# Residuals and norms handed over per stream, an output product by 128 tokens, and modulation as dot products on VectorE

## Chip, cores and metric

One core of one Trainium2 chip. The metric is the device time of one execution in microseconds, the median of several. Short names: PE is TensorE (PEld its weight loads), DVE is VectorE, ACT is ScalarE, POOL is GpSimd, SP is SyncE, whose queue issues nearly all the loads.

## The reference, cut to what matters

Two layers work on two streams of 256 tokens of width 1024: the context (stream 0 in the kernel) and the latent (stream 1). Each layer has a token mixer and a gated FFN with a width-3 convolution. Each of the two sub-layers is normed before and after, and modulated by six vectors of shift, scale and gate.

```python
sh1, sc1, g1, sh2, sc2, g2 = jnp.split((silu_c @ ada_w[layer] + ada_b[layer])[:, None, :], ADA_CHUNKS, axis=-1)
...
u_lat = rms_norm(h_lat, g_pre1) * (1.0 + sc1) + sh1
...
h_lat = h_lat + g1 * rms_norm(y_lat, g_post1)
v_lat = rms_norm(h_lat, g_pre2) * (1.0 + sc2) + sh2
h_lat = h_lat + g2 * rms_norm(conv_ffn(v_lat, w_ffn_in[layer], ...), g_post2)
```

The mixer ends in a product by w_out (1024x1024), the FFN in one by w_ffn_out (2816x1024). The context has the same chain with its own vectors; the second layer needs the context only as far as the mixer's keys and states, and has no FFN for it. The output is the latent stream.

## The kernel before

**Numbers and products.** Every f32 operand of a big product is split into a high part and a low part, and a product is three PE instructions (high by high, high by low, low by high). A chunk of weights is loaded by SP into one of five buffers called raw (line 246), copied by ACT to the high part wh (line 350), and the low part wl is formed by DVE (line 352); wh and wl have three buffers each. The casts are given with high priority. The kernel is written in a framework whose scheduler fixes each engine's instruction order ahead of the run, by priority (the order in which the program states the work, unless marked as urgent) and by when it reckons the operands ready. Each engine then works through its own list in that order.

**The token mixer's end.** `merge` (line 955) makes the merged tile mg. `outputs` (line 444) multiplies it by w_out in halves of 512 output columns: the first half for all streams together, then the second half stream by stream. In the second halves the last four k tiles are done token tile by token tile. Every weight chunk covers two k tiles. Lines 481 to 483 are the three instructions. After each half `post_half` (line 432) has ACT sum the squares (line 383) and DVE multiply by the gate row (line 436). The optional argument `fill` is a generator that is advanced once per weight chunk, in the first half only (line 455).

**Residual and norm.** In program order they come after all of `outputs`. `post_end` (line 438): POOL adds the two sums (line 441) and takes the power -1/2 (line 378), DVE adds the scaled result to the residual, 1024 columns at once (line 442). `norm_in` (line 414): ACT sums squares over 1024 columns (line 383), POOL adds and takes the power (lines 389, 378), ACT and DVE scale a half each into hn (lines 394, 395), and `prenorm` (line 397) has PE transpose it (line 405, urgent) into a PSUM bank for two column blocks, ACT write the modulated high part (line 409), DVE a copy of the modulated value (line 411), and DVE or POOL, in turn, the low part (line 412).

**The FFN.** `ffn_pair` (line 1006) is one of 22 column tiles. In the first layer the first three are done per stream with 256 tokens ("early pairs": context first, then its latent counterpart after the latent's norm), all the others for both streams at once. Then `outputs` does the FFN's own product, latent first. The context's FFN values are split in two when they are used (`inner`, line 1141): ACT the high part (line 1145), POOL the low part (line 1146).

**Modulation of later stages.** It has two forms. `ada_unit` (line 274) does 512 columns on PE: line 289, 128 columns at a time over 8 k tiles, then a copy, a transpose and small DVE steps (`ada_turn`). `ada_dots` (line 329) does one block of 128 columns per step: a load of 512 KB into a raw buffer and one DVE dot product per stream (line 338). One generator `ada` chains these. The first layer's runs through two units (the next layer's first shift), 8 + 8 blocks for the context and 8 + 32 for the latent; eight steps are taken before the early pairs, 2.7 per later pair, and the rest as `fill` in the FFN product. The second layer's is two units (its own last gate), all taken before its FFN.

**Between the layers.** `finish(1)` (line 1153) does the latent's residual and its norm for the next layer after the FFN product. `finish(0)` does the same for the context, called in the next layer after its first six projections, which need the latent only.

```python
        for g in groups:
            for t in range(2):
                self.post_end(*part[g, t], hs[g][t])
            self.norm_in(fp, l, g, hs[g], "A2", 24, v)
            for j in early:
                self.ffn_pair(l, fp, j, v, new(j), g * CTX, CTX, q0, True, j >= 2)
```

## Time and profile before

| what | value |
|---|---|
| median of 3 runs | 1571.18 us (1569.73 to 1573.08) |
| the profiled execution's own time | 1568.4 us |
| its span, first to last instruction | 1566.6 us |
| mean granted PE clock | 0.991 of full speed |
| PE busy | 1490.8 us, 95% |
| DVE busy | 1039.5 us, 66% |
| ACT busy | 738.4 us, 47% |
| POOL busy | 245.3 us, 16% |

The median carries what one can compare between kernels; the rows come from the one profiled execution, which was 2.8 us faster than the median. Its span leaves out 1.8 us of its own time. Positions in rows are microseconds from the span's start. The first layer's mixer output product is at 543 to 591, its FFN at 603 to 857, its FFN product at 857 to 986; the second layer's mixer output product is at 1328 to 1354, its FFN at 1367 to 1498, its FFN product at 1498 to 1559.

### The profile page before, as it was taken

The numbers are of one execution on the slowest core, as the hardware profiler recorded it, in microseconds if no ns is written. First come the engines' busy times: TensorE is split into PE (matmuls) and PEld (weight loads), VectorE is DVE, ScalarE is ACT, GpSimd is POOL, SyncE is SP. The second block draws the span as 40 slices with busy tenths as digits, with TensorE's granted clock in tenths as the row PEclk, the third lists the DMA queues.
The fourth block names the chain that finished last, engine by engine and source line by source line (L and its number), as shares of the span: only waits on it lengthen the run. The fifth ranks groups of instructions, "written<-read, shape, count | busy, mean of one in ns | idle before, by whom it ended". The sixth has DMA issues, their size and how long they took to land. (4 is left out here: it accounts for less than half of the span.)

```text
span 1566.6 us, 24172 instructions
## 1 busy us (share of the span) xinstructions
PE 1490.8 (95%) x9187; PEld 1279.0 (82%) x9187; DVE 1039.5 (66%) x1872; ACT 738.4 (47%) x1326; POOL 245.3 (16%) x335
## 2 busy tenths in 40 slices
PE   6999999999999998999999999899999989899997
PEld 5889877777777887888878886899997878799986
DVE  5546678778896457767776447646676787577754
ACT  3473334444444346332333346564455555455543
POOL 2101221001212223000000316401111123100000
PEclk9999999999999999999999999999999999899999
DMA  9321134333332356776665545422351334665553
GB/s 352 117 95 59 64 121 140 104 93 94 108 121 82 118 168 220 238 238 215 223 205 175 176 135 153 135 95 82 95 160 56 95 93 131 212 190 184 185 182 104
DMA packets 69717, 227.70 MB, mean 145 GB/s; under 512 B 7712, under 2 KB 8368, under 8 KB 69600
## 3 DMA queue, kind: packets, MB, share of 16 engines
q1 hardware_dynamic: 68000, 220.76, 43.9%
q0 software_dynamic: 1600, 5.39, 1.0%
q8 instruction: 72, 1.18, 0.3%
q14 instruction: 45, 0.37, 0.1%
HBM read 225.06 MB, written 1.06 MB: 144 GB/s over the span
## 5 line engine op out<-in xcount | busy, mean ns | idle before, releaser
L352 DVE TENSOR_TENSOR wl<-raw,wh 128x1024 fp32r<-128x1024 f32 (+6 forms) x333 | 385.7, 1163 | 181.5 <-ACT wh L350 180.0
L350 ACT CAST wh<-raw 128x1024 fp32r<-128x1024 f32 (+6 forms) x333 | 320.6, 966 | 239.0 <-PE mm L365 97.5
L364 PE MATMUL mm<-act,wh 128*128 128x256 f32 (+1 forms) x1096 | 372.7, 340 | 1.8 <-DVE ft L1020 1.6
L366 PE MATMUL mm<-act,wl 128*128 128x256 f32 (+1 forms) x1096 | 369.9, 338 | 4.2 <-DVE wl L352 4.1
L365 PE MATMUL mm<-act,wh 128*128 128x256 f32 (+1 forms) x1096 | 370.2, 338 | 0.2 <-POOL act L412 0.2
L366 PEld LDWEIGHTS mm<-act,wl 128*128 128x128 f32 x1096 | 209.5, 191 | 25.8 <-DVE wl L352 5.8
L364 PEld LDWEIGHTS mm<-act,wh 128*128 128x128 f32 x1096 | 209.7, 191 | 23.2 <-ACT wh L350 2.6
L365 PEld LDWEIGHTS mm<-act,wh 128*128 128x128 f32 x1096 | 209.7, 191 | 19.7 <-POOL act L412 0.4
L338 DVE CUSTOM_DVE_ANT_0 adot<-raw,srow,S 128x1024 bf16<-128x1024 f32 x104 | 134.0, 1289 | 73.5 <-DMA raw<-in_adat 67.4
L366 PE MATMUL ps<-act,wl 128*128 128x256 f32 (+1 forms) x328 | 109.3, 333 | 0.9 <-DVE wl L352 0.9
L364 PE MATMUL ps<-act,wh 128*128 128x256 f32 (+1 forms) x328 | 109.2, 333 | 0.0
L365 PE MATMUL ps<-act,wh 128*128 128x256 f32 (+1 forms) x328 | 109.2, 333 | 0.0
L483 PE MATMUL ps<-wh,al 128*128 128x512 f32 x198 | 78.8, 398 | 3.3 <-POOL al L1146 3.2
L579 PE MATMUL mm<-wh,act 128*128 128x272 f32 (+1 forms) x256 | 77.7, 304 | 1.6 <-ACT kb L770 1.6
L1022 ACT ACTIVATE ft<-ft 128x256 f32<-128x256 f32 (+1 forms) x47 | 23.7, 503 | 114.5 <-DVE ft L1020 90.4
L581 PE MATMUL mm<-wh,act 128*128 128x272 f32 (+1 forms) x256 | 77.0, 301 | 0.3 <-POOL act L412 0.3
L580 PE MATMUL mm<-wl,act 128*128 128x272 f32 (+1 forms) x256 | 76.8, 300 | 0.3 <-DVE wl L352 0.3
L1146 POOL TENSOR_TENSOR al<-ac,ah 128x256 fp32r<-128x256 f32 x44 | 41.7, 951 | 215.5 <-ACT ah L1145 215.4
L378 POOL TENSOR_TENSOR st<-st,mhalf 128x1 f32<-128x1 f32 (+3 forms) x56 | 48.8, 872 | 160.2 <-DVE st L606 123.5
L366 PEld LDWEIGHTS ps<-act,wl 128*128 128x128 f32 x328 | 62.6, 191 | 7.1 <-DVE wl L352 1.3
L364 PEld LDWEIGHTS ps<-act,wh 128*128 128x128 f32 x328 | 62.8, 191 | 6.0
L365 PEld LDWEIGHTS ps<-act,wh 128*128 128x128 f32 x328 | 62.6, 191 | 5.9
(300 smaller groups left out, 2830.5 us busy)
## 6 DMA issues: line engine op xcount, KB each, us to landing
raw<-in_wflat SPq DMA_DIRECT2D x253, 512.0 KB, 3.7
raw<-in_adat SPq DMA_DIRECT2D x80, 512.0 KB, 4.2
raw<-in_wflat SPq DMA_DIRECT2D x48, 256.0 KB, 2.7
araw<-in_ada SPq DMA_DIRECT2D x16, 512.0 KB, 7.2
raw<-in_ada SPq DMA_DIRECT2D x16, 512.0 KB, 3.9
raw<-in_wflat SPq DMA_DIRECT2D x8, 480.0 KB, 3.5
raw<-in_wflat SPq DMA_DIRECT2D x8, 408.0 KB, 3.2
raw<-in_wflat SPq DMA_DIRECT2D x8, 384.0 KB, 6.5
```

What stands on the lines that cost most here:

```text
L338: nc.vector.tensor_tensor_reduce(junk, r, rows[:, i], 1.0, self.S[l][:, L_AB + b:L_AB + b + 1], ALU.mult, ALU.add, self.MV[l][:, b, g:g + 1])
L350: nc.scalar.copy(h, raw)
L352: nc.vector.tensor_sub(lo, raw, h.bitcast(F32))
L364: self.nc.tensor.matmul(ps, a, xh(k), start=first and k == 0, stop=False)
L365: self.nc.tensor.matmul(ps, a, xl(k), start=False, stop=False)
L366: self.nc.tensor.matmul(ps, b, xh(k), start=False, stop=last and k == nk - 1)
L378: self.nc.gpsimd.tensor_tensor(r, ms, self.mhalf[:, :n], ALU.pow)
L483: self.nc.tensor.matmul(ps, xl, wh, start=False, stop=last)
L579: nc.tensor.matmul(ps, uh[:, k, tt], h[:, c], start=k == 0, stop=False)
L580: nc.tensor.matmul(ps, uh[:, k, tt], lo[:, c], start=False, stop=False)
L581: nc.tensor.matmul(ps, ul[:, k, tt], h[:, c], start=False, stop=k == KD - 1)
L1146: nc.gpsimd.tensor_sub(lo, a[k][0], h.bitcast(F32))
```

## The change

- `ada_unit` on PE is dropped. The first layer's generator has only dot products: 8 + 16 blocks for the context and 8 + 40 for the latent; none is taken before the early pairs, 2.5 per later pair, the rest as fill. The second layer's has its own 8 blocks for the latent, 0.5 per pair.
- `outputs` advances `fill` in the second halves too, and calls `done(g, ...)` as soon as a stream's second half is stated.
- `post_end` works in halves of 512 columns, each followed by a caller's step: the sum of squares of that half (`renorm`), or the store of that half (at the end).
- The first layer: the context's residual and normed tile are stated before the latent's second half, its transposes and modulation behind that half and before the latent's residual. Behind the FFN product the same, latent first; `finish()` only transposes and modulates the context.
- The second layer's mixer output product is done by `outputs_by_tile`: 128 tokens at a time, both halves; all eight chunks are loaded during tile 0, and seven of them have buffers of their own for wh and wl. Tile 0's normed tile is transposed (urgent) during tile 1 into four PSUM banks that tile 1 later completes.
- Of the context's low parts in the FFN product, the even k tiles go to DVE.

```diff
-    def weights(self, key, urgent=True):
+    def weights(self, key, urgent=True, pool=None):
...
-            h = self.wp.tile([P, WCH], F32R, tag="wh", name=self.nm("wh"))[:, :n]
+            new = lambda tag: (pool.tile([P, WCH], F32R, name=self.nm(tag)) if pool else self.wp.tile([P, WCH], F32R, tag=tag, name=self.nm(tag)))[:, :n]
+            h = new("wh")
             nc.scalar.copy(h, raw)
-            lo = self.wp.tile([P, WCH], F32R, tag="wl", name=self.nm("wl"))[:, :n]
+            lo = new("wl")
...
-    def post_end(self, s, yg, h):
+    def post_end(self, s, yg, h, after):
 
         ms = self.st(1)
         self.nc.gpsimd.tensor_scalar(ms, s[:, 0:1], s[:, 1:2], EPS, ALU.add, ALU.add)
-        self.nc.vector.scalar_tensor_tensor(h, yg, self.rstd(ms, 1), h, ALU.mult, ALU.add)
+        r = self.rstd(ms, 1)
+        for i in range(2):
+            c = slice(512 * i, 512 * i + 512)
+            self.nc.vector.scalar_tensor_tensor(h[:, c], yg[:, c], r, h[:, c], ALU.mult, ALU.add)
+            after(i, c)
+
+    def renorm(self, tp, s, yg, h):
+
+        q, ms = self.st(2), self.st(1)
+        self.post_end(s, yg, h, lambda i, c: self.square_sums(tp.tile([P, 512], F32, tag="ft", name=self.nm("jq"), bufs=2), h[:, c], q[:, i:i + 1]))
+        self.nc.gpsimd.tensor_scalar(ms, q[:, 0:1], q[:, 1:2], EPS, ALU.add, ALU.add)
+        hn = tp.tile([P, D], F32, tag="yg", name=self.nm("hn"), bufs=4)
+        self.scaled(hn, self.rstd(ms, 1), h)
+        return hn
...
-                if i == 0:
-                    next(fill, None)
+                next(fill, None)
...
+            done(g, [part[g, t] for t in range(2)])
+
+    def outputs_by_tile(self, key, x, tp, wp, gain, fill, done):
+
+        ws = {}
+        for t in range(2):
+            s, yg = self.st(2), tp.tile([P, D], F32, tag="yg", name=self.nm("yg"), bufs=4)
+            for i in (t, 1 - t):
+                y = self.mm()
+                for k in range(0, KD, 2):
+                    if t == 0:
+                        ws[i, k] = self.weights((*key, i, k), pool=wp if (i, k) != (1, KD - 2) else None)
+                        next(fill, None)
+                    for j in range(2):
+                        self.tokens_proj(y, [a[:, t * P:(t + 1) * P] for a in x(k + j)], [a[:, 512 * j:512 * j + 512] for a in ws[i, k]], k + j == 0, k + j == KD - 1)
+                self.post_half(tp, y, gain(), i, s, yg)
+            done(t, s, yg)
...
+        def wo_done(g, part):
+            if g:
+                for m in range(0, KD, 2):
+                    self.prenorm(fp, l, (m, m + 1), {0: hn[0]}, "A2", 24, v)
+            hn[g] = [self.renorm(fp, *part[t], hs[g][t]) for t in range(2)]
+
+        def tile_done(t, s, yg):
+            h = self.renorm(fp, s, yg, hs[1][t])
+            if t == 0:
+                hn[1] = [self.ps() for _ in range(KD // 2)]
+            for i, ps in enumerate(hn[1]):
+                self.turned(ps, (2 * i, 2 * i + 1), h, t)
...
-        for _ in range(8 if full else 12):
-            next(ada, None)
+        dots = lambda bs, g: self.ada_dots(fp, bs, (g,))
+        second = [(l, b) for b in range(40, 48)]
+        ada = chain(*(dots(second + [(l + 1, b) for b in range(40 if g else 16)], g) for g in range(2))) if full else dots(second, 1)
...
-                due += 2.7 if j < NF - 2 else 0
+                due += (2.5 if full else 0.5) if j < NF - 2 else 0
...
-            nc.gpsimd.tensor_sub(lo, a[k][0], h.bitcast(F32))
+            (nc.gpsimd if k % 2 else nc.vector).tensor_sub(lo, a[k][0], h.bitcast(F32))
...
+        def fo_done(g, part):
+            if not full:
+                for t in range(2):
+                    self.post_end(*part[t], hs[g][t], lambda i, c: nc.sync.dma_start(self.d["out"][t * P:(t + 1) * P, c], hs[g][t][:, c]))
+                return
+            hn[g] = [self.renorm(fp, *part[t], hs[g][t]) for t in range(2)]
+            if g:
+                normed(g)
+
+        def normed(g):
+            for m in range(0, KD, 2):
+                self.prenorm(fp, l + 1, (m, m + 1), {g: hn[g]}, "A1", 0, u)
+
+        def finish():
+            normed(0)
+            fst.close()
```

## Rows read from the trace of the kernel before

**Rows 1.** The page's head: span, and PE's busy time and share.

```profile
span 1566.6 us, 24172 instructions
...
PE 1490.8 (95%) x9187; PEld 1279.0 (82%) x9187; DVE 1039.5 (66%) x1872; ACT 738.4 (47%) x1326; POOL 245.3 (16%) x335
```

**Rows 2.** Busy time by stretch (length, engines, clock, DMA, GB/s), first layer, behind its output product.

```profile
591.00:603.50 12.50, 8.49 (x154) 6.32 (x147) 9.20 (x18) 9.32 (x19) 5.22 (x9) 1.00 0.83 301
603.50:622.20 18.70, 16.77 (x130) 15.45 (x128) 17.30 (x29) 13.66 (x21) 5.35 (x6) 1.00 0.60 194
622.20:641.00 18.80, 17.54 (x143) 17.26 (x144) 14.44 (x22) 8.79 (x15) 2.35 (x2) 1.00 0.67 204
```

**Rows 3.** PE's timeline there (start, length, instruction, count).

```profile
590.34 0.40 PE L483 MATMUL ps<-wh,mg 128*128 128x512 f32 x1
590.66 2.15 PE L289 MATMUL ps<-raw,scol 128*32 128x128 f32 x66
592.75 1.57 PE L405 MATMUL ps<-ident,hn 128*128 128x128 f32 x12
...
603.50 0.36 PE L364 MATMUL mm<-act,wh 128*128 128x256 f32 x1
```

**Rows 4.** ACT's timeline there: context scaled, context modulated.

```profile
588.68 0.72 ACT L394 ACTIVATE hn<-hC,st 128x512 f32<-128x512 f32 x1 [0.99 <-POOL st L378]
...
596.90 1.91 ACT L409 ACTIVATE act<-ps,MV,A 128x256 fp32r<-128x256 f32 x4
```

**Rows 5.** The page's groups (count, busy us, mean ns, idle before): the dot product.

```profile
L338 DVE CUSTOM_DVE_ANT_0 adot<-raw,srow,S 128x1024 bf16<-128x1024 f32 x104 | 134.0, 1289 | 73.5 <-DMA raw<-in_adat 67.4
```

**Rows 6.** Tile al, the FFN values' low parts (ns min/median/max, first and last start).

```profile
L1146 POOL TENSOR_TENSOR al<-ac,ah x44: 721/740/1797, 616.8 to 983.5; 128x256 fp32r<-128x256 f32 x44
...
L357 DVE TENSOR_TENSOR al<-ft,al x44: 415/421/426, 633.6 to 1501.0; 128x256 fp32r<-128x256 f32 x44
```

**Rows 7.** Busy time by stretch: the FFN product's second halves, second layer's start.

```profile
919.00:945.00 26.00, 26.00 (x113) 20.94 (x112) 12.57 (x11) 9.75 (x11) 0.00 (x0) 1.00 0.59 182
945.00:986.00 41.00, 37.74 (x163) 27.70 (x162) 28.30 (x30) 28.03 (x52) 30.42 (x38) 1.00 0.51 156
986.00:1014.00 28.00, 23.38 (x184) 23.10 (x182) 20.76 (x33) 17.24 (x33) 11.85 (x19) 0.94 0.38 113
```

**Rows 8.** PE's waits (us in total, times, longest): transposes waiting for a scaled tile.

```profile
PE ps L405 <- ACT hn L394: 7.0, 2, 4.6
```

**Rows 9.** POOL's timeline at the second layer's start: the norm's add.

```profile
991.69 2.51 POOL L389 TENSOR_SCALAR st<-st 128x1 f32<-128x1 f32 x1
```

**Rows 10.** Chain that ended last, second layer, behind its output product (start, length, what).

```profile
1353.75 0.24 PE ps L483
1354.08 0.70 ACT junk L383 x2
...
1355.25 0.57 POOL st L378
...
1359.75 0.23 POOL st L389
...
1360.66 0.50 DVE hn L395
1361.20 2.82 PE ps L405 x12
...
1369.12 0.58 PE mm L366
```

**Rows 11.** Busy time by stretch, second layer: output product's start, FFN's start, the rest.

```profile
1327.50:1333.00 5.50, 3.86 (x10) 2.85 (x10) 5.32 (x6) 3.09 (x5) 2.37 (x2) 0.70 0.69 228
1366.80:1374.00 7.20, 5.67 (x25) 5.37 (x26) 7.19 (x12) 3.57 (x5) 2.20 (x3) 0.50 0.74 247
1374.00:1498.00 124.00, 124.00 (x1035) 124.00 (x1035) 87.86 (x132) 69.70 (x109) 0.74 (x1) 1.00 0.59 184
```

**Rows 12.** The chain's last link: the residual before the last store.

```profile
1560.62 1.28 DVE hL L442
```

More of the change, by code (lines that the diff above doesn't have):

```diff
@@ L324, in ada_gains @@
             nc.vector.tensor_tensor(self.G[l]["G1" if kind == 2 else "G2"][:, m0:m1, :], mv, gain(1 if kind == 2 else 3), ALU.mult)
-    def ada_units(self, l, units):
-        return chain(*(self.ada_unit(l, ((512 * i, 512),)) for i in units))
     def ada_dots(self, pool, blocks, streams):
@@ L412, in prenorm @@
             (nc.gpsimd if i % 2 else nc.vector).tensor_sub(dst[1][:, m, c], t, dst[0][:, m, c].bitcast(F32))
-    def norm_in(self, tp, l, g, hs, k, boff, dst):
-        hn = [tp.tile([P, D], F32, tag="yg", name=self.nm("hn"), bufs=4) for _ in hs]
-        for t in range(2):
-            self.scaled(hn[t], self.rms(hn[t], hs[t]), hs[t])
-        for m in range(0, KD, 2):
-            self.prenorm(tp, l, (m, m + 1), {g: hn}, k, boff, dst)
     def gate_rows(self, fp, l, k, g):
@@ L436, in post_half, with outputs @@
         self.nc.vector.tensor_mul(yg[:, c], y, gain[:, c])
-    def post_end(self, s, yg, h):
+    def post_end(self, s, yg, h, after):
         ms = self.st(1)
         self.nc.gpsimd.tensor_scalar(ms, s[:, 0:1], s[:, 1:2], EPS, ALU.add, ALU.add)
-        self.nc.vector.scalar_tensor_tensor(h, yg, self.rstd(ms, 1), h, ALU.mult, ALU.add)
-    def outputs(self, key, nk, x, tp, gains, order, fill=iter(())):
+        r = self.rstd(ms, 1)
[10 more added lines that the diff above has]
+        return hn
+    def outputs(self, key, nk, x, tp, gains, order, fill, done):
         y, part = {}, {}
@@ L475, in outputs @@
             half(1, (g,))
-        return part
+            done(g, [part[g, t] for t in range(2)])
[13 more added lines that the diff above has]
+            done(t, s, yg)
     def tokens_proj(self, ps, x, w, first, last):
@@ L1108, in layer @@
         at = lambda g: slice(g * CTX - q0, (g + 1) * CTX - q0)
-        part = self.outputs((l, "wo"), KD, lambda g, k: (mg[0][:, k, at(g)], mg[1][:, k, at(g)]), fp, rows, groups, gains())
+        x = lambda g, k: (mg[0][:, k, at(g)], mg[1][:, k, at(g)])
+        hn = {}
+        def wo_done(g, part):
[9 more added lines that the diff above has]
+                self.turned(ps, (2 * i, 2 * i + 1), h, t)
+        if full:
+            self.outputs((l, "wo"), KD, x, fp, rows, groups, gains(), wo_done)
+        else:
+            with pool("wo", far) as wp:
+                self.outputs_by_tile((l, "wo"), partial(x, 1), fp, wp, lambda: rows[1], gains(), tile_done)
         mst.close()
-        ada = chain(self.ada_units(l + 1, range(2)), *(self.ada_dots(fp, [(l, b) for b in range(40, 48)] + [(l + 1, b) for b in range(8, 40 if g else 16)], (g,)) for g in range(2))) if full else self.ada_units(l, range(10, 12))
-        for _ in range(8 if full else 12):
-            next(ada, None)
+        dots = lambda bs, g: self.ada_dots(fp, bs, (g,))
+        second = [(l, b) for b in range(40, 48)]
+        ada = chain(*(dots(second + [(l + 1, b) for b in range(40 if g else 16)], g) for g in range(2))) if full else dots(second, 1)
         ast = ExitStack()
@@ L1123, in layer @@
         for g in groups:
-            for t in range(2):
-                self.post_end(*part[g, t], hs[g][t])
-            self.norm_in(fp, l, g, hs[g], "A2", 24, v)
+            for m in range(0, KD, 2) if g else ():
+                self.prenorm(fp, l, (m, m + 1), {1: hn[1]}, "A2", 24, v, None if full else hn[1][m // 2])
             for j in early:
@@ L1145, in inner @@
             nc.scalar.copy(h, a[k][0])
-            nc.gpsimd.tensor_sub(lo, a[k][0], h.bitcast(F32))
+            (nc.gpsimd if k % 2 else nc.vector).tensor_sub(lo, a[k][0], h.bitcast(F32))
             return h, lo
-        part = self.outputs((l, "fo"), NF, inner, fp, rows, groups[::-1], ada)
+        def fo_done(g, part):
[12 more added lines that the diff above has]
+            fst.close()
+        self.outputs((l, "fo"), NF, inner, fp, rows, groups[::-1], ada, fo_done)
         run(ada)
         ast.close()
-        def finish(g):
-            for t in range(2):
-                self.post_end(*part[g, t], hs[g][t])
-                if not full:
-                    nc.sync.dma_start(self.d["out"][t * P:(t + 1) * P, :], hs[g][t])
-            if full:
-                self.norm_in(fp, l + 1, g, hs[g], "A1", 0, u)
-            if g == groups[0]:
-                fst.close()
-        finish(1)
+        if not full:
+            fst.close()
+            return None, None
         return u, finish
```

33 lines of the change are left out of this document (10 added, 23 removed).

## The prediction, made before the change was run

> **What bounds the kernel now.** First the head of the page: TensorE (PE) is busy for 1490.8 of 1566.6 us [rows 1]. So time is won in two ways only: where PE stands still, and where PE does work that another engine could do. A table of busy time by stretch then shows where PE stands still around the edit. There are four places: behind the first layer's output product (8.49 of 12.50 us busy, then 16.77 of 18.70 and 17.54 of 18.80) [rows 2], in the last part of its FFN product (37.74 of 41.00) and behind it (23.38 of 28.00) [rows 7], behind the second layer's output product [rows 10, 11], and the end [rows 12]. The reader should see in the timelines that all of these are the same thing: residual, norm, transposes and modulation run as a chain of small steps on ScalarE (ACT), VectorE (DVE) and GpSimd (POOL), and PE waits for its end.
>
> **First layer, behind the output product (dropped PE modulation; context norm ahead of the latent's end).** The last product starts at 590.34, the first FFN product at 603.50 [rows 3]. The context's normed tile was begun at 588.68, so it was ready before the product ended, but its first modulated tile was written only at 596.90 [rows 4], because its transposes came at 592.75, behind 66 rows of modulation products [rows 3]. From 591 to 641, 50 us, PE must do 6 early pairs of 48 products at 0.12 us (124 us for 1035 [rows 11]), 34.6 us; 32 transposes at 1.57/12 = 0.13 [rows 3], 4.2 us; and 128 modulation rows at 2.15/66 = 0.033 [rows 3], 4.2 us. That leaves 7.0 us of waits. The change takes the 4.2 away, since the 16 blocks become dot products on DVE. With the context's transposes free to run beside the latent's last products, I let somewhat less than half of the waits go, 2.8 us: DVE, 17.30 of 18.70 us busy here [rows 2], keeps the rest alive, because the same latent norm must be done beside the same weight splits. **Gain 7 us.** Bounds: 2 (the waits grow by 2.2 because DVE, not PE, is what ends last) and 11 (all waits go).
>
> **FFN of both layers.** The first layer's FFN gets 42 dot products where it had 45, which I cost at nothing. In the second, 8 new dots of 1.29 us [rows 5], 10.3 us, lie beside 124 us in which DVE is busy for 87.86 and PE is never idle [rows 11]: nothing, and if that cover were gone, 10 us. The loads are hidden too: 24 more column-block loads for 16 weight loads that go, 8 more in all on SP's queue, in stretches where the DMA engines are busy for 0.59 to 0.67 [rows 2, 11]. One more broadcast of the silu row goes out on POOL's queue, before an FFN in which POOL is busy for 0.74 us.
>
> **The first layer's FFN product, and the start of the second layer.** This is where the change adds work. Of 72 dots 42 are handed out in the FFN; 30 follow, one per weight chunk, 11 in the first half, 9 in the latent's second half, 10 in the context's. Half of the 22 context splits also move from POOL to DVE there: 11 at 0.42 us (the same shape on L357, median 421 ns [rows 6]), 4.6 us; on POOL they took 740 ns, at worst 1797 [rows 6]. From 919 to 945 DVE goes from 12.57 to 12.57 + 9 x 1.29 = 24.2 of 26 us; from 945 to 986 from 28.30 to 28.30 + 12.9 + 4.6 = 45.8 of 41; from 986 to 1014 it had 20.76 of 28 [rows 7]. Together 90.8 us of DVE in a stretch of 95. Dots must slip out of the middle part into the last, and they hold raw buffers of the weights' ring of 5 while they wait; queued behind them on DVE are the weights' low parts, for which PE waits. PE needs only 26.00 + 37.74 + 23.38 = 87.1 us [rows 7], so DVE becomes the limit. Where DVE was at its fullest beside this kind of work it reached 17.30/18.70 = 92.5% [rows 2]: 90.8/0.925 = 98.2, a loss of 3.2. At 100% it is a gain of 4.2. I take the middle. **Gain 0.5**, bounds -14 (a share of 0.83, below) and 6.
>
> **Second layer, output product by 128 tokens.** Before, the chain after the last product (1353.75) runs both tiles' residuals, squares and scalings in turn on the same three engines, the second normed half ends at 1361.16, PE's transposes take until 1364, and the FFN goes steadily only from 1369.12 [rows 10]. After, tile 0 is done during tile 1's products: 48 at 0.24 us [rows 10], 11.5 us, against a chain of about 6. What stays exposed is tile 1's chain alone: square 0.35 (0.70 for two), POOL's add 0.23 and power 0.57, residual 1.28 in halves [rows 12], the second half's square 0.35, add and power again 0.80, scaling 0.50 [rows 10], with 0.3 at the start and some 0.1 between steps: 5.2 us. With two transposes and one modulated tile (another 1.5) the FFN begins at about 1360.8 in place of 1366.8. Before, PE did 25 products in the 7.2 us to 1374 [rows 11], worth 3.0 us, as though FFN had begun at full speed at 1371.0; this run-in loss of 4.2 us I leave as it is, since the granted clock there is 0.50 (1.2 GHz) after the slack time and would be after 7 us of slack too. **Gain 5.5.** Bounds: 0.5 and 8. The low one is the other side of the change: tile 0 wants all 8 chunks in 11.5 us, one per 1.4 us, where a chunk before lasted 2.8. At the product's start PE already lost time to the splits (3.86 of 5.50 us busy at clock 0.70, DVE 5.32 [rows 11]); a second such loss is 5 us. Seven chunks with tiles of their own can be split ahead, so I take it near the top.
>
> The Trainium skill, page "TensorE: Matmul & The Clock Gate", section "What's actually happening", says that the throttled clock is the default and that activity releases it. That speaks against taking PE's filler work out of the wait; by it alone the run-in could lengthen by part of the 7.2 us. The trace has the clock at 0.50 in spite of that filler [rows 11], so I leave the sum.
>
> **End.** The residual is cut in halves and its store with it: the last store starts after the same 1.28 us [rows 12], but carries half. **Gain 0.5**, bounds 0 and 1.5.
>
> **Sum.** 7 + 0.5 + 5.5 + 0.5 = 13.5 us less one: the split of each residual and square in two adds a fixed part to each, on chains that are exposed three times, bounded by 0 and 2. 12.5 us off the profiled execution's 1568.4 gives 1555.9; that execution lies 2.8 below the median of 1571.18, so on the median 1558.7, **1559**.
>
> **The rivals.**
> *A. The dots fit.* DVE runs full without starving PE, and the waits behind both products go: 11 + 6 + 5.5 + 0.5 = 23, 1548. For it: DVE's demand is still below the stretch's 95 us. Against: 92.5% is the most that rows show. Chance 0.17.
> *B. POOL is held up.* POOL's add of one column takes 0.23 us at 1359.75 [rows 10] and 2.51 us at 991.69 [rows 9], beside a busy DVE; PE then waited 4.6 us for a normed tile [rows 8], its transposes being already ahead in its queue. If four more chains (each has four POOL steps) lose 2.3 us once, 9.2 us go: gain 3.3, 1568. For it: DVE gets fuller in two of the four. Chance 0.17.
> The Trainium skill, page "SBUF — State Buffer", section "SBUF: two separate sides", says that DVE with two SBUF inputs and a GpSimd instruction that reads SBUF exclude each other for a whole instruction. The 2.51 us agrees with it; that the dots hold POOL so is shown by no run yet.
> *C. DVE starves PE in the FFN product: slower.* Place: 919 to 1014. If waiting dots keep raw buffers, weights arrive late and DVE idles too; at a share of 0.83 the stretch lasts 109 us, 14 more, and with the other gains at their low ends (2 + 0.5) the time is 1583; it decides from a stretch longer than 95 + 12 = 107 us, with the other terms as forecast. Chance 0.09.
> *D. The order changes nothing.* The scheduler hoists ready work by itself already, and only the 4.2 us of PE products go, 1567. Against: the context's transposes sat behind other work for 4 us. Chance 0.07.
>
> **Numbers.** Forecast 0.5, A 0.17, B 0.17, C 0.09, D 0.07. What a measurement of this kernel can tell is about 0.2%, 3 us. Faster: forecast, A, D and three quarters of B, with a little off each: 0.82. Within 0.2%: the rest of B and some of the forecast's edge, 0.09. Slower: C, 0.09. The range leaves out C and the far ends: 1547 to 1570.
>
> **What would show it.** Right: no modulation products on PE; first FFN product within 5 us of the first layer's output product, and within 8 us of the second's; POOL no longer named before L483's counterpart; DVE above 90% from the latent's second half to the next layer. Wrong: PE waiting there for the weights' low parts or for dots' loads; transposes waiting for normed tiles for over 3 us at more places than before; the second layer's output product longer than 27 us.

## The result, and the profile after

The changed kernel took 1586.59 us (median of 4 runs, 1582.89 to 1589.02) beside 1570.45 for the kernel before. The ratio is 1.0107, with a 95% interval of 1.0088 to 1.0126: 1.1% slower, where 1559 was forecast. The profiled execution took 1588.27 us.

The page's head, after (beside [rows 1]):

```profile
span 1586.5 us, 23749 instructions
...
PE 1492.2 (94%) x8927; PEld 1277.2 (81%) x8927; DVE 1076.5 (68%) x1945; ACT 742.3 (47%) x1346; POOL 219.5 (14%) x314
```

260 PE instructions are gone, and yet PE is busy for 1.4 us more, since some of the others ran at a lower clock. DVE has 37 us more to do. The 128 dots there are in the page's groups (beside [rows 5]), and the FFN values' low parts, now on two engines (beside [rows 6]):

```profile
L315 DVE CUSTOM_DVE_ANT_0 adot<-raw,srow,S 128x1024 bf16<-128x1024 f32 x128 | 165.4, 1292 | 81.4 <-DMA raw<-in_adat 75.7
```

```profile
L1171 DVE TENSOR_TENSOR al<-ac,ah x22: 410/424/965, 621.9 to 1003.2; 128x256 fp32r<-128x256 f32 x22
L1171 POOL TENSOR_TENSOR al<-ac,ah x22: 737/748/1533, 626.6 to 1004.0; 128x256 fp32r<-128x256 f32 x22
```

To see where the time went, I cut both profiled executions at the same products (first and last PE product that reads the merged tile, the FFN values, or the second layer's decay). Lengths in us; the last column is the best of the later kernels:

| stage | before | after | best (no. 18) |
|---|---|---|---|
| start to first output product (code the same) | 543.8 | 545.9 | 543.6 |
| first output product | 46.5 | 51.1 | 47.3 |
| to the FFN product | 264.7 | 262.9 | 264.6 |
| FFN product | 130.7 | 146.1 | 130.6 |
| to the second layer's decay | 52.5 | 51.5 | 51.8 |
| to the second output product | 289.7 | 295.8 | 289.7 |
| second output product | 25.7 | 26.4 | 25.7 |
| to the second FFN product | 145.0 | 140.2 | 142.4 |
| second FFN product | 59.8 | 59.7 | 59.8 |
| end | 8.2 | 6.9 | 6.9 |

The loss is 15.4 us in the first layer's FFN product, 6.1 ahead of the second output product and 4.6 in the first, of which some 2 are the context's 16 transposes (0.13 us each), which ran behind that product before; 4.8 come back in the second layer's FFN. The stretch ahead of the first output product holds the same code in all kernels and lies between 543.4 and 547.6 in those run here, so a difference of two us in one stage is no evidence.

Busy time by stretch, after (columns as in [rows 2]: length, PE, PEld, DVE, ACT, POOL, clock, DMA):

```profile
597.20:643.30 46.10, 39.05 (x282) 36.72 (x281) 35.05 (x57) 27.55 (x49) 10.68 (x14) 0.89 0.42 136
925.00:955.00 30.00, 29.31 (x123) 22.46 (x122) 24.58 (x31) 11.21 (x13) 0.75 (x1) 1.00 0.85 294
955.00:1006.00 51.00, 39.95 (x157) 29.79 (x156) 44.13 (x63) 28.81 (x55) 18.16 (x26) 0.90 0.71 237
1006.00:1034.00 28.00, 24.33 (x187) 23.85 (x186) 20.95 (x36) 18.17 (x37) 9.07 (x20) 0.94 0.42 127
1380.00:1400.50 20.50, 13.74 (x82) 12.96 (x81) 10.82 (x19) 8.54 (x18) 4.66 (x8) 0.75 0.09 32
1400.50:1519.00 118.50, 118.26 (x986) 118.05 (x985) 92.53 (x143) 68.83 (x106) 0.00 (x0) 1.00 0.71 218
```

925 to 1034 answers to [rows 7]: it lasts 109 us where 95 were needed, and DVE is busy for 24.58 + 44.13 + 20.95 = 89.7 of them. DVE is fuller, but not full, and unevenly so:

```profile
961.00:978.00 17.00, 11.25 (x39) 8.07 (x40) 15.42 (x26) 9.27 (x19) 4.59 (x8) 0.72 0.54 179
978.00:992.00 14.00, 13.09 (x54) 9.78 (x52) 13.75 (x18) 7.79 (x14) 6.05 (x6) 0.98 0.78 258
```

From 961 to 992 it is busy for 29.2 of 31 us. What PE waits for is in its list of waits (beside [rows 8]; us in total, times, longest):

```profile
PE ps L379 <- ACT hn L372: 9.3, 4, 3.9
PE ps L379 <- DVE hn L373: 8.8, 4, 6.3
...
PE mm L487 <- DVE sig L973: 4.1, 1, 4.1
...
PE ps L487 <- DVE nt L396: 3.5, 1, 3.5
```

L379 is the transpose of a normed tile: 18.1 us of waits, beside 7.8 before. The longest, 6.3, stands behind the second output product, where that chain became shorter and PE has no modulation products left to do beside it; 5.0 (3.87 and 1.17) stand in the FFN product. Here is the largest loss, in PE's timeline behind the latent's last FFN product, and then in DVE's:

```profile
956.88 0.40 PE L489 MATMUL ps<-wh,al 128*128 128x512 f32 x1
961.15 0.75 PE L379 MATMUL ps<-ident,hn 128*128 128x128 f32 x4 [3.87 <-ACT hn L372]
...
963.84 0.63 PE L489 MATMUL ps<-wh,al 128*128 128x512 f32 x1
965.64 1.53 PE L379 MATMUL ps<-ident,hn 128*128 128x128 f32 x12 [1.17 <-DVE hn L373]
970.71 0.47 PE L487 MATMUL ps<-wh,ah 128*128 128x512 f32 x1 [3.54 <-DVE nt L396]
...
974.40 0.80 PE L489 MATMUL ps<-wh,al 128*128 128x512 f32 x1 [0.89 <-DVE al L1171]
...
978.41 0.51 PE L489 MATMUL ps<-wh,al 128*128 128x512 f32 x1
```

```profile
965.50 1.28 DVE L315 CUSTOM_DVE_ANT_0 adot<-raw,srow,S 128x1024 bf16<-128x1024 f32 x1
...
966.82 1.28 DVE L315 CUSTOM_DVE_ANT_0 adot<-raw,srow,S 128x1024 bf16<-128x1024 f32 x1
...
968.03 0.54 DVE L396 TENSOR_SCALAR nt<-ps,A,MV 128x256 f32<-128x256 f32 x1
968.49 1.28 DVE L315 CUSTOM_DVE_ANT_0 adot<-raw,srow,S 128x1024 bf16<-128x1024 f32 x1
```

The reader should see three things. The latent's transposes stand in PE's list directly behind the latent's own last product and ahead of the context's products, so PE stands still for the whole residual and norm. Then the context's product needs a PSUM bank that DVE's copies nt must empty, and three dots stand ahead of and between these copies. And after the waits, instructions last 0.63 us in place of 0.39. The four waits are 9.5 us. Busy time over the whole product, before and then after, gives the account:

```profile
855.00:985.70 130.70, 126.55 (x546) 99.54 (x545) 67.54 (x74) 62.90 (x108) 49.13 (x59) 1.00 0.51 157
```

```profile
859.90:1006.00 146.10, 131.41 (x546) 101.98 (x544) 99.38 (x137) 63.97 (x112) 27.68 (x37) 0.96 0.63 209
```

PE stands for 14.7 us in place of 4.2, and its 546 instructions take 4.9 us more: 10.5 and 4.9 make the 15.4.

The second loss is in DVE's timeline ahead of the second output product:

```profile
1344.42 4.63 DVE L330 TENSOR_TENSOR wl<-raw,wh 128x1024 fp32r<-128x1024 f32 x4
...
1352.84 0.75 DVE L973 SCALAR_TENSOR_TENSOR sig<-sig,mm 128x256 f32<-128x256 f32 x2
```

Four urgent splits of the output product's chunks go ahead of the merge's own step and two more between its later ones, PE's bank stays held until the step at 1352.84, and PE stands for 4.1 us.

### The profile page after: what moved, and what is told of

It is laid out like the page before. It is cut to its first block, busy times and chain, and to the rows that moved or that the text cites. A ratio compares the mean times of both kernels' runs of the same rounds, so it can differ in the third digit from the quotient of the medians.

```text
span 1586.5 us, 23749 instructions
## 1 busy us (share of the span) xinstructions
PE 1492.2 (94%) x8927; PEld 1277.2 (81%) x8927; DVE 1076.5 (68%) x1945; ACT 742.3 (47%) x1346; POOL 219.5 (14%) x314
## 5 line engine op out<-in xcount | busy, mean ns | idle before, releaser
L315 DVE CUSTOM_DVE_ANT_0 adot<-raw,srow,S 128x1024 bf16<-128x1024 f32 x128 | 165.4, 1292 | 81.4 <-DMA raw<-in_adat 75.7
L974 POOL TENSOR_TENSOR acc<-acc,sig 128x512 f32<-128x512 f32 (+1 forms) x32 | 44.9, 1406 | 111.8 <-DVE sig L973 111.8
```

What stands on the lines that cost most here:

```text
L315: nc.vector.tensor_tensor_reduce(junk, r, rows[:, i], 1.0, self.S[l][:, L_AB + b:L_AB + b + 1], ALU.mult, ALU.add, self.MV[l][:, b, g:g + 1])
L974: nc.gpsimd.tensor_add(acc[:, d, :], acc[:, d, :], s)
```

## Experiments

All ran in 3 rounds against the kernel before. The parts that were taken back, alone and together:

| part | short name |
|---|---|
| the second output product's splits not urgent | calm |
| first layer's modulation as before (16 blocks on PE, dots offered in the product's first half only) | old modulation |
| first layer's residuals and norms stated where they stood | old order |
| squares written into the tile they come from, not into the FFN pairs' buffers | own squares |
| all of the context's low parts on POOL | low on POOL |
| second output product by the old `outputs` | old product |

| no. | kernel | us | ratio (95%) |
|---|---|---|---|
| 1 | dots in first half only | 1589.75 | 1.0121 (1.0094 to 1.0149) |
| 2 | all norms behind all halves | 1589.31 | 1.0128 (1.0100 to 1.0157) |
| 4 | old product | 1581.04 | 1.0074 (1.0051 to 1.0098) |
| 6 | calm | 1581.06 | 1.0072 (1.0047 to 1.0096) |
| 7 | calm, low on POOL | 1583.02 | 1.0095 (1.0060 to 1.0131) |
| 8 | calm, old modulation | 1586.19 | 1.0107 (1.0089 to 1.0126) |
| 9 | calm, old order | 1595.62 | 1.0162 (1.0138 to 1.0187) |
| 10 | calm, old modulation, old order | 1580.28 | 1.0068 (1.0049 to 1.0086) |
| 11 | as 10, own squares | 1568.57 | 0.9992 (0.9978 to 1.0006) |
| 12 | as 11, new modulation | 1585.05 | 1.0081 (1.0051 to 1.0112) |
| 13 | calm, own squares alone | 1583.93 | 1.0085 (1.0058 to 1.0113) |
| 14 | as 11, low on POOL | 1566.59 | 0.9980 (0.9966 to 0.9994) |
| 15 | as 12, dots in first half only | 1578.22 | 1.0056 (1.0035 to 1.0076) |
| 16 | as 11, its dots in both halves | 1569.20 | 0.9997 (0.9985 to 1.0008) |
| 17 | as 11, new order | 1585.46 | 1.0098 (1.0073 to 1.0123) |
| 18 | as 14, old product | 1566.54 | 0.9980 (0.9970 to 0.9990) |
| 19 | as 17, moved transposes not urgent | 1581.58 | 1.0082 (1.0050 to 1.0114) |
| 20 | before, with two second-layer parts | 1566.60 | 0.9976 (0.9962 to 0.9991) |

### The FFN product, first attempts (1, 2)

```diff
-                next(fill, None)
+                if i == 0:
+                    next(fill, None)
...
-                due += (2.5 if full else 0.5) if j < NF - 2 else 0
+                due += (3.6 if full else 0.5) if j < NF - 2 else 0
```

> The dot products go out in the FFN (3.6 per pair in place of 2.5) and in the first half of the FFN product only, as before; all else as changed. Theory D (the 20 dots in the second halves fill VectorE, and TensorE waits for what is queued behind them): the first layer's FFN product, 146 us in the changed kernel and 131 before, comes back to 131 to 134; 12 to 15 us off, 1572 to 1575. Theory O (the order: urgent transposes stand in TensorE's list right behind the stream's last product and wait there for the normed tile): the waits for normed tiles, 18 us in all, stay; 2 to 5 us off, 1582 to 1585.

Measured 1589.75: FFN product 141.4 (4.7 less), FFN stage 269.9 (7.0 more). Neither theory's time came. In no. 2, `done` is called for all streams after the last second half:

> Residuals and norms are stated after all of a product's halves again; dots and all else as changed. Theory O: TensorE's waits for normed tiles fall from 18 us to some 8 to 10 as before (7.8), and the half-speed stretches behind them go; 8 to 13 us off, 1574 to 1579. Theory D: VectorE has the same work in the same place; within 3 us, 1584 to 1590.

Measured 1589.31: FFN product 141.0, but the way to the decay 58.5, 7.0 more, and the first output product still 51.1. Both moved the loss and did not remove it.

### The second output product (4, 6)

```diff
...
-        if full:
+        if True:
             self.outputs((l, "wo"), KD, x, fp, rows, groups, gains(), wo_done)
...
```

> The second layer's output product as before (first half, then second half, both token tiles), residual and norm behind it in the new halves; all else as changed. If the product by 128 tokens is worth what its end shows (some 5 us sooner to the FFN) and costs nothing else: 1590 to 1592. If what it gains behind it is given back at its start (TensorE waited 4.2 us for a bank held by the merge, whose VectorE step was queued behind four urgent weight splits): 1585 to 1588, no difference. If it costs more than it gains: below 1584.

```diff
-                        ws[i, k] = self.weights((*key, i, k), pool=wp if (i, k) != (1, KD - 2) else None)
+                        ws[i, k] = self.weights((*key, i, k), urgent=False, pool=wp if (i, k) != (1, KD - 2) else None)
```

> The changed kernel with the eight weight splits of the second layer's output product not marked urgent. Theory U (the urgent splits, set free by buffers of their own, pass the merge's last steps on VectorE): the 4.2 us wait at the product's start goes, and with the short half-speed stretch behind it 3 to 6 us, 1581 to 1584. Rival (tile 0 is starved by its splits anyway, one per 1.4 us): the wait moves into tile 0, 1586 to 1590.

Both take 5.5 us off (1581.04, 1581.06). The stage ahead of the product is 289.8 and 290.4 again (before 289.7). In no. 6 the merge's step comes between the splits and PE's wait for it is gone, in DVE's timeline:

```profile
1341.32 2.36 DVE L330 TENSOR_TENSOR wl<-raw,wh 128x1024 fp32r<-128x1024 f32 x2
1343.61 0.75 DVE L977 SCALAR_TENSOR_TENSOR mg<-acc,mg 128x256 fp32r<-128x256 f32 x2
1344.28 0.74 DVE L973 SCALAR_TENSOR_TENSOR sig<-sig,mm 128x256 f32<-128x256 f32 x2
```

So the urgency of the splits is shown as the cause of this loss. It also shows that the form by 128 tokens gives nothing by itself: from the decay to the second FFN product it is 290.4 + 27.7 + 140.6 = 458.7, with the old product 456.6.

### Modulation, order and low parts (7 to 10)

```diff
-        ada = chain(*(dots(second + [(l + 1, b) for b in range(40 if g else 16)], g) for g in range(2))) if full else dots(second, 1)
+        ada = chain(self.ada_units(l + 1, range(2)), *(dots(second + [(l + 1, b) for b in range(8, 40 if g else 16)], g) for g in range(2))) if full else dots(second, 1)
+        for _ in range(8 if full else 0):
+            next(ada, None)
...
```

```diff
         def wo_done(g, part):
-            if g:
-                for m in range(0, KD, 2):
-                    self.prenorm(fp, l, (m, m + 1), {0: hn[0]}, "A2", 24, v)
-            hn[g] = [self.renorm(fp, *part[t], hs[g][t]) for t in range(2)]
+            parts[g] = part
...
         for g in groups:
-            for m in range(0, KD, 2) if g else ():
+            if full:
+                hn[g] = [self.renorm(fp, *parts[g][t], hs[g][t]) for t in range(2)]
+            for m in range(0, KD, 2):
...
```

> The changed kernel with calm splits (as in the run before this one that had them, 1581.1) and with all low halves of the FFN product's context operand on POOL again. If VectorE's queue, made longer by these 416 to 426 ns pieces (16 of the 32), is what starves TensorE there: the product falls from 147 to about 140 us and the time to 1574. If they only trade one wait for another (3.2 us of waits for POOL's pieces before, 2.8 us for VectorE's after): 1580 to 1582.

> Calm splits, and the first layer's stage with the modulation as it was: 16 streams' blocks back from VectorE dots to TensorE, the dots offered in the product's first half alone; the order of the residuals, the halves and the low parts stay new. If the dots are the cause of the product's 15 us: the product is back near 132 us, the FFN loses the 2 us of TensorE's steps, time about 1569 to 1572. If the order of residuals and norms is the cause: product still 141 or more, and the time 1578 to 1583.

> Calm splits, modulation new, but the residuals and norms of the first layer are given to the scheduler where they stood before: each stream's just ahead of its FFN pairs, and after the FFN product for the latent, after the next layer's first projections for the context; the second layer stays by 128 tokens. If the order is the cause: the output product back from 51 to 46.5 us, the FFN product to about 133, time 1563 to 1567. If the dots are: output product 46.5 (its transposes no longer stand in it), FFN product still 141 to 147, time 1574 to 1578.

> Both: calm splits, modulation of the first layer and order of its residuals as before. What is left of the change is the residual, squares and stores in halves, the split low parts, the second layer's dots and its product by 128 tokens. If dots and order hold the whole loss: 1563 to 1567, that is 2 to 6 us under the kernel before by the second layer's shorter stages (5 us) and end (1.3 us). If the halves or the low parts are the cause instead: 1575 or more.

Measured 1583.02, 1586.19, 1595.62 and 1580.28. Nos. 7 to 9 lie above every time that was expected of them; no. 10 lies where the halves or the low parts were to be the cause. No. 10 has the FFN product back (130.9 us) but an FFN stage of 280.4, beside 264.7 before; no. 9 has 271.7. The reason is in ACT's timeline of no. 10 (L384 sums squares):

```profile
622.49 0.62 ACT L384 ACTIVATE jq<-hL 128x512 f32<-128x512 f32 x1
...
627.21 0.63 ACT L384 ACTIVATE jq<-hL 128x512 f32<-128x512 f32 x1 [1.15 <-DVE hL L446]
```

These are the latent's squares, 30 us behind its product. Their scratch tile jq takes its turn in the two buffers (ft) through which the FFN pairs rotate. With the old order, the context's three early pairs stand ahead of them in the program and hold these buffers. So nos. 9 and 10 tested two things at once.

### The parts apart (11 to 17)

```diff
-        self.post_end(s, yg, h, lambda i, c: self.square_sums(tp.tile([P, 512], F32, tag="ft", name=self.nm("jq"), bufs=2), h[:, c], q[:, i:i + 1]))
+        self.post_end(s, yg, h, lambda i, c: self.square_sums(yg[:, c], h[:, c], q[:, i:i + 1]))
```

> The run with the old modulation and the old order, and the squares of each residual written into the dead product tile it came from, not into the two buffers that the FFN pairs rotate through. In that run the latent's four squares waited behind the context's first three FFN pairs (622.49 and 627.21 us, beside 592.38 and 595.86 in the kernel before), and the FFN stage took 280.4 us, beside 264.7. If the shared buffers are the cause: FFN stage 264 to 267 us, time 1563 to 1567, 3 to 6 us under the kernel before. If the halved residual itself or chance in the schedule is: FFN stage 275 or more, time 1575 to 1581.

Measured 1568.57 (1.6 above the time expected), FFN stage 266.7: the shared buffers are shown to be the cause of that stage's loss in no. 10. ACT's timeline has the squares at the product's end:

```profile
592.05 0.63 ACT L384 ACTIVATE yg<-hL 128x512 f32<-128x512 f32 x1 [1.87 <-DVE hL L446]
...
597.15 0.63 ACT L384 ACTIVATE yg<-hL 128x512 f32<-128x512 f32 x1 [1.39 <-DVE hL L446]
```

No. 11 is the base for the rest: level with the kernel before, though it keeps the halves, the low parts on two engines and the second layer's parts.

> The run with the old order alone (all modulation as dots, calm splits), with the squares in tiles of their own. If the 16 added blocks of dots are the cause of the FFN product's loss: output product 46 to 47 us and FFN stage 262 to 267 again, but FFN product and the way to the next layer still 8 to 16 us over the kernel before: 1572 to 1580. If the order is the cause: 1562 to 1566.

> The changed kernel with calm splits and nothing else but the squares in tiles of their own. In the changed kernel the squares come ahead of the FFN pairs in the program, so by the shared-buffer theory little is to be had there: 1578 to 1582, as with calm splits alone (1581.1). If the two buffers also hold up the FFN product's latent chain (first transposes 5.1 us behind the squares): 1573 to 1577.

> As the first run of this call, and all low parts of the FFN product's context operand on POOL, as before. If they are worth what the prediction gave them (3.2 us of waits for POOL's pieces in the kernel before, against the waits for VectorE's): 0 to 3 us slower than the first run. If VectorE's 16 pieces cost as much as they give: the same within 1.5 us.

("The first run" there is no. 11.) No. 12 took 1585.05: the new modulation alone costs 16.5 us, more than was expected. Its profiled execution was the fastest of its four, 1578.69, so its stages show less: FFN product and way to the decay 138.0 + 59.2 = 197.2, beside 183.6 in no. 11. Busy time by stretch in the product's end, no. 11 and then no. 12:

```profile
955.00:990.00 35.00, 31.82 (x143) 24.02 (x142) 27.58 (x39) 24.57 (x49) 17.11 (x26) 1.00 0.52 167
```

```profile
955.00:993.00 38.00, 32.36 (x131) 24.69 (x132) 35.10 (x47) 21.59 (x39) 18.16 (x18) 0.91 0.82 277
993.00:1025.00 32.00, 23.09 (x161) 22.25 (x160) 21.20 (x37) 17.68 (x36) 11.09 (x23) 0.84 0.29 94
```

DVE is busy for 35.10 of 38 us there, and the normed tiles come late. The first output product was to be 46 to 47 us again, and is 51.1, as in nos. 9 and 15. No dot runs there (the first is at 634.1). In PE's timeline the context's transposes stand inside the product as in the changed kernel, with the same waits, though no. 12 states them behind it:

```profile
584.23 0.55 PE L379 MATMUL ps<-ident,hn 128*128 128x128 f32 x3 [0.90 <-ACT hn L372]
...
588.73 1.32 PE L379 MATMUL ps<-ident,hn 128*128 128x128 f32 x9 [1.15 <-DVE hn L373]
```

So without PE's modulation products the scheduler places these transposes early by itself, and 3.8 us of the new modulation's cost are not the dots'. No. 13 (own squares with both new parts) took 1583.93: the buffers were not what held up the changed kernel. No. 14 took 1566.59, 2.0 less than no. 11, where 0 to 3 more or no change was expected. The ten times of each overlap, and no. 7 took 2.0 more than no. 6 for the same edit: that the even low parts on DVE cost or save anything is not shown.

> As the run with all modulation as dots, the old order and squares of their own (product and the way to the next layer 197.2 us together, beside 183.6 with the old modulation), but the dots are offered at 3.6 per FFN pair and in the product's first half only, none in its second. If where the dots stand is the cause: product and way to the next layer 182 to 186 us, FFN stage at most 5 us longer, time 1566 to 1571. If their number is: at least 193 us for the two, or an FFN stage 8 us or more longer: 1574 to 1580.

> The kernel with the old modulation, the old order and squares of their own (1568.6), with no dot added: only 2.2 steps per FFN pair instead of 2.7, and steps offered in both halves of the FFN product. If dots in the product's second half are the cause by their place: the product and the way to the next layer together 4 to 10 us longer, time 1572 to 1578. If it is the number of dots: within 2 us of 1568.6.

> The kernel with the old modulation and squares of their own (1568.6), with the changed order of residuals and norms. If the order costs by itself: first output product 51 instead of 47.3 us and FFN product with the way to the next layer 188 to 193 instead of 183.6, time 1573 to 1583. If the order only meets the dots (nothing crosses it where VectorE has room): 1567 to 1571; if it brings what the prediction gave it for the first output product: 1560 to 1564.

> The best kernel so far (old modulation and order in the first layer, squares of their own, low parts on POOL; 1566.6) with the second layer's output product as it was, not by 128 tokens. If the product by 128 tokens gives what the prediction gave it: 4 to 6 us slower, 1571 to 1573. If, as the stages of the two runs with and without it say, it gives nothing once its splits are calm (456.6 and 457.9 us from the next layer's start to the FFN's end): 1564.5 to 1567.5.

No. 16 took 1569.20: the place of the dots costs nothing (0.6). No. 15 took 1578.22: product and way to the decay are 183.2 again, but the FFN stage is 269.9, and the first output product 51.0. With the old order and the new modulation the kernel loses 10 to 16 us, and the place of the dots decides where. In no. 15 the FFN stage holds 66 dots in place of no. 12's 47, and PE waits there for the weights' low parts, which DVE forms (PE's waits, no. 15 and then no. 12):

```profile
PE ps L344 <- DVE wl L330: 9.3, 8, 2.4
```

```profile
PE ps L344 <- DVE wl L330: 0.9, 3, 0.4
```

So here the 16 more dots of 1.3 us are free in neither place. No run changes their number and leaves PE's modulation products in.

No. 17, the order alone, took 1585.46: 16.9 us, in the first output product (+3.6), the FFN stage (+5.5) and the FFN product (+8.4). PE's timeline in no. 17, and the busy time behind it (beside 1.00 for the clock in no. 11's row above):

```profile
962.25 0.40 PE L513 MATMUL ps<-wh,al 128*128 128x512 f32 x1
967.15 1.11 PE L402 MATMUL ps<-ident,hn 128*128 128x128 f32 x4 [4.50 <-ACT hn L395]
```

```profile
967.00:982.00 15.00, 11.90 (x35) 9.26 (x36) 7.83 (x14) 7.99 (x17) 3.65 (x7) 0.50 0.11 38
```

```profile
960.00:1008.00 48.00, 40.55 (x159) 31.78 (x158) 29.39 (x42) 28.93 (x55) 15.32 (x26) 0.82 0.42 129
```

In no. 11 most of these transposes come after some 45 products of the context, and wait for 1.30:

```profile
963.09 0.39 PE L513 MATMUL ps<-wh,al 128*128 128x512 f32 x1
964.77 1.20 PE L402 MATMUL ps<-ident,hn 128*128 128x128 f32 x9 [1.30 <-ACT hn L395]
```

No. 17 and no. 13 differ by the modulation alone, and are alike. The new modulation costs 16.5 us with the old order and nothing with the new; the order costs 16.9 with the old modulation and nothing with the new. The stages show where they don't add:

| stage | neither (11) | order (17) | modulation (12) | both (13) |
|---|---|---|---|---|
| first output product | 47.3 | 50.9 | 51.1 | 51.1 |
| to the FFN product | 266.7 | 272.2 | 260.4 | 264.7 |
| FFN product | 130.8 | 139.2 | 138.0 | 145.5 |
| to the second layer's decay | 52.8 | 52.6 | 59.2 | 52.8 |

In the FFN product they nearly do: 8.4 and 7.2 alone, 14.7 together. In the first output product either one puts the transposes into the product, so its cost comes once. On the way to the decay the new modulation costs 6.4 us with the old order and nothing with the new; why the order brings these back is not settled. (No. 12's execution lies 6.4 us under its median.)

### Urgency, and a version that beats both (18 to 20)

```diff
-        with self.tc.high_priority():
+        with self.tc.high_priority() if urgent else nullcontext():
...
-                    self.prenorm(fp, l, (m, m + 1), {0: hn[0]}, "A2", 24, v)
+                    self.prenorm(fp, l, (m, m + 1), {0: hn[0]}, "A2", 24, v, urgent=False)
...
```

> As the run with the changed order alone (1585.5), but the transposes of the two streams that are moved forward (the context's in the first output product, the latent's in the FFN product) are no longer marked urgent; all others stay urgent. In that run the latent's transposes stand right behind the latent's last product, TensorE waits 4.5 us for them at 962.65 and runs at 0.82 from 960 to 1008. If the urgent place in TensorE's in-order queue is what the order costs: first output product 47 us, FFN product 131 to 133, time 1567 to 1573. If it is the earlier residual and norm work on VectorE and ScalarE: 1580 to 1586.

Measured 1581.58, 3.9 us less than no. 17, which the spread of four executions each hardly separates. The first output product is 47.3 again, but the FFN product 138.5, with the wait where it was:

```profile
964.52 1.11 PE L402 MATMUL ps<-ident,hn 128*128 128x128 f32 x4 [4.49 <-ACT hn L395]
```

The urgency explains the first output product's 3.6 of the 17 us. Behind the FFN product the statement itself, ahead of the context's half, puts the transposes there. A finer cut of the remaining 13 was not tried.

No. 18 took 1566.54, as no. 14: the product by 128 tokens gives nothing.

```diff
-        ada = chain(self.ada_units(l + 1, range(2)), *(self.ada_dots(fp, [(l, b) for b in range(40, 48)] + [(l + 1, b) for b in range(8, 40 if g else 16)], (g,)) for g in range(2))) if full else self.ada_units(l, range(10, 12))
-        for _ in range(8 if full else 12):
+        ada = chain(self.ada_units(l + 1, range(2)), *(self.ada_dots(fp, [(l, b) for b in range(40, 48)] + [(l + 1, b) for b in range(8, 40 if g else 16)], (g,)) for g in range(2))) if full else self.ada_dots(fp, [(l, b) for b in range(40, 48)], (1,))
+        for _ in range(8 if full else 0):
...
-                due += 2.7 if j < NF - 2 else 0
+                due += (2.7 if full else 0.5) if j < NF - 2 else 0
...
```

> The kernel before with two parts of the change alone, both in the second layer: its eight remaining blocks of modulation as VectorE dots at one per two FFN pairs, and the last residual and store in halves. The prediction's terms for these: 1.3 to 5 us for the FFN stage and the end; in the earlier runs the second layer's FFN stage took 142.4 us with its old output product, beside 145.0, and the end 6.9, beside 8.2. If these stages stand by themselves: 1565.5 to 1568, about 4 us under the kernel before. If they come from the product by 128 tokens or from the low parts: 1568.5 or more.

No. 20 (with the last residual and store in halves too) took 1566.60, FFN stage 143.0, end 6.9. Nos. 14, 18 and 20 beat both kernels, by 0.2% over the one before. What they share, beside the old modulation and order of the first layer, is the second layer's eight dots, the end, and the low parts on POOL as before.

## Why the prediction was wrong

**First layer, "Gain 7".** The step that failed is "with the context's transposes free to run beside the latent's last products, I let somewhat less than half of the waits go". Output product and FFN stage went from 311.2 to 314.0, outside the bounds. The transposes did run there, but they waited (0.88 and 1.14 us) at the head of PE's queue, and the product grew by 4.6. Then the first FFN products waited 3.27 us for the context's own modulated tile. Its low part, on POOL, stands behind three steps of the latent's norm (PE's timeline, and then POOL's):

```profile
605.29 0.58 PE L343 MATMUL mm<-act,wh 128*128 128x256 f32 x1 [3.27 <-POOL act L397]
```

```profile
601.86 1.24 POOL L430 TENSOR_SCALAR st<-st 128x1 f32<-128x1 f32 x1 [1.40 <-ACT jq L361]
...
604.51 0.72 POOL L397 TENSOR_TENSOR act<-nt,act 128x256 fp32r<-128x256 f32 x1
```

The sign for being right came all the same: the first FFN product starts 0.2 us behind the last output product (597.20 and 597.0), since the transposes' time had moved into that product. The 4.2 us of dropped PE work came as 2.5 (311.5 in no. 12, in its fastest execution, 314.0 in no. 11), and the order took 9.1 (323.1 in no. 17).

**FFN product, "Gain 0.5".** This was the largest miss: from 183.2 to 197.6 us with the way to the decay, 14.4 where the low bound was 14. The sum of DVE's work was right (90.8 forecast, 89.7 measured), and the stretch of 95 became 109, the length that rival C gave it. But "I take the middle" between shares of 92.5% and 100% failed: the share was 0.82. The forecast spread DVE's work evenly over the stretch. Measured, DVE idled for 9.1 us while it waited for weights' high parts from ACT and for 8.5 in the norm's own steps, and was full (29.2 of 31 us) from 961 to 992, where the chain needed it. C's mechanism, raw buffers held by waiting dots, is not what the waits show: only 0.7 us of PE's waits there are for weights. They show rival B's half sentence, the transposes "already ahead in its queue" (5.0 us), and C's heading in another way: dots ahead of the copies that free PE's bank (3.5) and low parts of FFN values late on DVE (2.4). That C's time, 1583, lies near the measured one is in part luck, since the other gains that it counted did not come.

**Second output product, "Gain 5.5".** The step that failed is "seven chunks with tiles of their own can be split ahead, so I take it near the top". They were split ahead, of the merge's steps too, and that cost 5.5 us. Without it the form gives nothing. The exposed chain did shrink, from 12.8 us (1354.0 to 1366.8) to 8.7 (1380.1 to 1388.8; the forecast's sum is 6.7), but the product lasted 2.0 longer than before in no. 6, and the slow run-in stayed: clock 0.75 from 1380 to 1400.5. The eight dots that I cost at nothing gave 2.0 to 2.6 (143.0 and 142.4 for 145.0), since two units of PE work went.

**End, "Gain 0.5".** It was 1.3, inside its bounds. **Halves, "less one":** nos. 18 and 20 differ by the first layer's halves, with squares of their own, and are level (1566.54 and 1566.60). In the old order and with the shared buffers they cost 11.7 us (nos. 10 and 11), which the term did not foresee.

**Rival B** did not come about where the loss is: POOL's additions for the norm took 0.32 and 0.39 us at 959.38 and 964.03 in the changed kernel. The longest of their kind is the 1.24 us at 601.86 above, beside a split on DVE from 601.72 to 602.93: some 0.9 us, ahead of the 3.27 us wait.

```profile
959.38 0.32 POOL L430 TENSOR_SCALAR st<-st 128x1 f32<-128x1 f32 x1 [2.44 <-ACT jq L361]
...
964.03 0.39 POOL L430 TENSOR_SCALAR st<-st 128x1 f32<-128x1 f32 x1 [2.36 <-ACT jq L361]
```

**D**, that the order changes nothing, was wrong the other way: it costs.

**The clock.** I left the sum as it was in face of a rule. The rows show two long waits that are paid for again: behind the 4.50 us wait of no. 17 the clock is 0.50 (1.2 GHz) from 967 to 982 and 0.82 in the mean of 48 us, where no. 11 has 1.00; behind the 3.87 us wait of the changed kernel it is 0.72 from 961 to 978. The Trainium skill's page "TensorE: Matmul & The Clock Gate", section "What's actually happening", says that activity releases the throttle; with this the trace agrees (no. 17 has 1.00 again from 982 to 1008, with PE busy throughout). But that the filler's absence would lengthen the run-in is not borne out: from the second layer's first FFN product on, the clock of 7.2 us is 0.50 with the modulation products (before, 1366.8 to 1374) and 0.61 without (no. 18, with the same output product, 1365 to 1372.2).

## What to carry to other kernels

Before a step is stated earlier, ask where its instructions will stand in the queue of the engine that bounds the kernel: a transpose that is queued ahead of independent products turns a hidden chain into a wait, and the lowered clock behind it costs more (4.9 us beside 10.5 us of added waits here). Taking work away can do the same, since a scheduler may then move urgent steps forward. Scratch tiles that share a ring with other work, and urgent casts, are such queues too, and can be seen as a step that runs long after its operands are ready. Work moved to an engine that is two thirds busy is not free where that engine feeds the critical chain: look at how busy it is just where the chain needs it, not in the mean.

## What the runs showed of the hardware

The granted clock was lower behind a stall: in no. 17 PE was busy for 0.65 of the 5 us from 962 to 967, and the clock was 0.50 for the next 15 us, in which PE was busy for 11.90, the same product's instructions lasting 0.63 us and not 0.39. A one-column addition on POOL took 0.30 to 1.24 us in one kernel (ten of L430), the longest beside a split on DVE that ended 0.17 us before it. And an order of instructions alone, with the same work on every engine, was worth 17 us, or 1.1% (nos. 11 and 17).
